# Attention values kept in DRAM by head pair, and the first value bands loaded ahead of the biases, in a hybrid encoder block

## The chip, the core and the metric

The kernel runs on one core of one Trainium2 chip. The metric is device time in microseconds (us); lower is better. A profiled execution of the same program gives the rows shown below; its span goes from the first to the last instruction.

## What is computed

The reference is one encoder block over 1024 tokens (a grid of 16 rows by 64 columns) of 1024 channels, in float32. Cut to what matters here:

```python
h = rmsnorm(x, norm_mix_g)
proj = h @ w_in                        # 1024 x 2048: u (512), q, k, v (512 each)
a = pool_mixer(u, w_pool, pool_scale)  # four groups of 128 channels
b = neighbourhood_attention(q, k, v, rpb)   # 8 heads of 64 channels
x = x + concat([a, b]) @ w_out
h = rmsnorm(x, norm_mlp_g)
x = x + square(relu(h @ w_up)) @ w_down
return rmsnorm(x, final_g)
```

In the attention each token at (row, column) attends to a window of 8 rows by 16 columns. The columns are worked in four bands of 16 query columns, whose keys and values lie in 24, 32, 32 and 24 grid columns.

## The kernel before

Every matmul is split in three: an operand is cut into a high part (a cast on ScalarE, line 100) and a low part (a subtraction on VectorE or GpSimd, line 101), and high x high, high x low and low x high go to TensorE (lines 143, 145 and 147). A weight tile therefore costs casts on ScalarE (`wh`) and subtractions on GpSimd (`wl`) before TensorE can use it.

The stages, in order of time: the norm of eight blocks of 128 tokens with the projection of the values, which `project_v` copies out of PSUM (`vs`, line 245) and stores to `vd` in DRAM; the bias tables `di` and `df`, built in SBUF and stored to DRAM; the projection of q and k for head pair 0 (`project_qk`, 24 matmuls for each half of the tokens, 96 in all); then a loop over 64 attention tiles in which TensorE works on the scores, the transposes and the values of one tile and, in between, on the projections of head pairs 1 to 3 and of the four pooling groups. After that come the output projection and the MLP, which the change doesn't touch.

`load_v(hp, j)` loads the values of head pair `hp` in band `j`: 96 or 128 partitions (4 grid rows of 24 or 32 columns) by four blocks of rows by 128 channels. `split_v` casts them into `vhl` on ScalarE and GpSimd. `load_bias` fills a bias tile with two loads; the first four tiles are eight loads, 240 and 160 KB or 300 and 120 KB for each tile. `fetch` loads a projection weight of 128 columns (512 KB), and `loaded` hands out one weight, puts the splitting of the next into the list `later`, and fetches the one after that.

All these loads are issued by SyncE (SP) on one queue. The projections use two PSUM banks in turn, so the third half-projection can't start before the first is out of its bank, and so on. What comes out is written by ScalarE (line 467 for q, line 476 for k) and VectorE (lines 468 and 477).

Up to the output projection the order on each engine isn't the order of the code: a list scheduler decides it when the program is built. Each engine then works strictly in that order, so an instruction that waits holds up all that stand behind it on its engine. SP has eight completion semaphores for its loads and uses them in turn: a load waits until the eighth load before it has landed.

Of the kernel before, what the change touches and what calls it, by code (L numbers as in the profile page):

```python
# [8 lines left out]
F32 = mybir.dt.float32  # L9
# [6 lines left out]
P = 128  # L16
T = 1024
# [3 lines left out]
HALF = 512  # L21
WINDOWS = (2, 4, 8, 16)
GW = 64
# [14 lines left out]
def block_kernel(ctx, tc, x, norm_mix_g, w_in, w_pool, pool_scale, rpb, w_out,  # L38
                 norm_mlp_g, w_up, w_down, final_g, out):
    nc = tc.nc  # L40
# [7 lines left out]
    out = out[0]  # L48
# [5 lines left out]
    dram = ctx.enter_context(tc.tile_pool(name="dram", bufs=1, space=DRAM))  # L54
# [12 lines left out]
    def bank(tag):  # L67
        return psum[0].tile([P, 512], F32, tag=tag, name=f"ps_{tag}")

    def t2(name, dt=F32):  # L70
        return k2.tile([P, 512], dt, tag="k2", name=name)

    def t4(name, dt=F32):
        return k4.tile([P, 1024], dt, tag="k4", name=name, bufs=NARROW)

    def t4w(name, n=1040):
        return k4.tile([P, 1152], F32, tag="k4w", name=name, bufs=WIDE)[:, :n]
# [4 lines left out]
    def r32(ap):  # L82
        return ap.bitcast(F32)
# [14 lines left out]
    def split(hi, lo, src, lo_eng=None):  # L98

        nc.scalar.copy(out=hi, in_=src)  # L100
        (lo_eng or nc.vector).tensor_tensor(out=lo, in0=src, in1=r32(hi), op=ALU.subtract)  # L101
# [38 lines left out]
    def three(ps, wh, wl, ah, al, first, last, more=False):  # L140


        nc.tensor.matmul(ps, wh, ah, start=first, stop=False, skip_group_check=more)  # L143
        yield
        nc.tensor.matmul(ps, wh, al, start=False, stop=False, skip_group_check=more)  # L145
        yield
        nc.tensor.matmul(ps, wl, ah, start=False, stop=last, skip_group_check=more)  # L147
        yield
# [3 lines left out]
    def step(k):  # L152

        if later and k % 4 == 0:
            later.pop(0)()
# [5 lines left out]
    def run(steps):  # L161
        for k, _ in enumerate(steps):
            step(k)
# [1 line left out]
    def quads(ts):  # L165
        return [t.rearrange("p (c t) -> p c t", c=4) for t in ts]

    vd = dram.tile([T, HALF], F32, name="vd")
    ad = dram.tile([T, D], F32, name="ad")
    di = dram.tile([8, 5, 16, KR, WSUM], F32, name="di")  # L170
    df = dram.tile([8, 8, 16, 8, WSUM], F32, name="df")
# [19 lines left out]
    with ExitStack() as pv:  # L191
# [24 lines left out]
        for i in range(4):  # L216
            raw = (t4w("wvraw", 1024) if i < WIDE else t4("wvraw")).rearrange("p (c n) -> p c n", c=2)
# [19 lines left out]
        def project_v(tt):  # L237
            tsl = slice(tt * P, (tt + 1) * P)
            ps = bank("pp")
            for c in range(NC8):  # L240
                g, k = divmod(c, 4)
                run(three(ps, hh[g][:, k, tsl], hl[g][:, k, tsl], wvh[:, c, :], wvl[:, c, :],
                          c == 0, c == NC8 - 1))
            vs = t2("vs")
            nc.scalar.copy(out=vs, in_=ps)
            nc.sync.dma_start(out=vd[tsl, :], in_=vs)

        transposed(norm_x(0), hh, hl, 0, ("S", "T"))
        for nh, ps in enumerate(gps):
# [52 lines left out]
        def loaded():  # L302

            flush()
            w = weights.pop(0)
            if weights:
                pieces(*weights[0], 2, nc.gpsimd)
            if cols:
                weights.append(fetch(cols.pop(0)))
            return w  # L310

        hn = norm_x(1)
        for tt in range(NC8):
            if tt + 1 < NC8:
                transposed(hn, hh, hl, (tt + 1) * P, ("S", "T"))
            if tt + 2 < NC8:
                hn = norm_x(tt + 2)
            project_v(tt)
            if tt == 3:
                build_tables()  # L320
            if tt == 3:
                weights.append(fetch(cols.pop(0)))
            if tt == 5:
                pieces(*weights[0], 2, nc.gpsimd)
                flush()
            if tt == 5:
                store_tables()

    def project(w, pss, chunks=range(NC8), blocked=False):

        for th, ps in pss:
            sl = slice(th * HALF, (th + 1) * HALF)
            for c in chunks:
                g, k = divmod(c, 4)
                ah, al = hh[g][:, k, sl], hl[g][:, k, sl]
                if blocked:
                    ah = ah.rearrange("p (r j c) -> p j r c", r=8, j=4)
                    al = al.rearrange("p (r j c) -> p j r c", r=8, j=4)
                yield from three(ps, w[0][:, c, :], w[1][:, c, :], ah, al, c == 0, c == NC8 - 1)
# [69 lines left out]
    with ExitStack() as pt_:  # L409
# [11 lines left out]
        def load_bias(h, e, rb):  # L421
            bt = bias[e, rb]
            if rb == 0:
                nc.sync.dma_start(out=bt[64:128], in_=di[h, 0:4].rearrange("s b r c -> (s b) r c"))
                nc.sync.dma_start(out=bt[0:64, 0:8, :], in_=df[h, 0:4].rearrange("s b r c -> (s b) r c"))
            else:
                nc.sync.dma_start(out=bt[0:80], in_=di[h].rearrange("s b r c -> (s b) r c"))
                nc.sync.dma_start(out=bt[80:128, 4:12, :], in_=df[h, 5:8].rearrange("s b r c -> (s b) r c"))

        def load_v(hp, j):  # L430
            c0, w, _ = BANDS[j]
            raw = t2("vraw").rearrange("p (c n) -> p c n", c=4)
            for c in range(4):
                src = bass.AP(vd.tensor, vd.offset + (c * 4 * GW + c0) * HALF + hp * P,
                              [[GW * HALF, 4], [HALF, w], [1, P]])
                nc.sync.dma_start(out=raw[:4 * w, c, :], in_=src)
            return raw

        def split_v(raw, j):
            w = BANDS[j][1]  # L440
            vhl = t4("vhl", F32R).rearrange("p (c s d) -> p c s d", c=4, s=4)
            split(vhl[:4 * w, :, 0:4:3, :], vhl[:4 * w, :, 1:3, :],
                  raw[:4 * w].rearrange("p c (e d) -> p c e d", e=2), lo_eng=nc.gpsimd)
            return vhl

        def tq(name):
            return qk.tile([P, T], F32R, tag="qk", name=name)

        def side(e):
            return slice(64 * e, 64 * e + 64), slice(64 - 64 * e, 128 - 64 * e)  # L450
# [3 lines left out]
        def project_qk(hp, loaded, last_first=False):  # L454
            kl = [tq("kl") for _ in range(2)]
            q1 = [tq("q1") for _ in range(2)]
            k1 = [tq("k1") for _ in range(2)]
            ready[hp] = q1, k1, kl
            wgt = loaded()
            for th in range(2):  # L460
                ps = bank("pp")
                yield from project(wgt, [(th, ps)], blocked=True)
                for e in range(2):
                    me, ot = side(e)
                    psj = ps[me].rearrange("p (j n) -> p j n", j=4)
                    q5 = q1[e].rearrange("p (j b n) -> p j b n", j=4, b=2)
                    nc.scalar.mul(out=q5[me, :, th], in_=psj, mul=-0.125)
                    nc.vector.scalar_tensor_tensor(  # L468
                        out=q5[ot, :, th], in0=psj, scalar=-0.125,
                        in1=r32(q5[me, :, th]), op0=ALU.mult, op1=ALU.subtract)  # L470

            def evac(th, ps):
                sl = slice(th * HALF, (th + 1) * HALF)
                for e in range(2):
                    me, ot = side(e)
                    nc.scalar.copy(out=k1[e][me, sl], in_=ps[me])
                    nc.vector.tensor_tensor(out=kl[e][me, sl], in0=ps[me],
                                            in1=r32(k1[e][me, sl]), op=ALU.subtract)
                    nc.sync.dma_start(out=r32(k1[e][ot, sl]), in_=r32(k1[e][me, sl]))
                    nc.sync.dma_start(out=r32(kl[e][ot, sl]), in_=r32(kl[e][me, sl]))  # L480

            wgt = loaded()
            if last_first:
                pss = [(th, bank("pp")) for th in range(2)]
                yield from project(wgt, pss, range(4))
                yield from project(wgt, pss, range(4, NC8))
                for th, ps in pss:
                    evac(th, ps)
            else:
                for th in range(2):  # L490
                    ps = bank("pp")
                    yield from project(wgt, [(th, ps)])
                    evac(th, ps)

        tiles = [(hp, j, e, rb) for hp in range(4) for j in range(4) for e in range(2) for rb in range(2)]
        bs, vraw, vhls, state = [], {}, {}, {}
# [149 lines left out]
            flush()  # L646
            yield from out_pools()

        for e in range(2):
            for rb in range(2):  # L650
                load_bias(e, e, rb)
        run(project_qk(0, loaded))
        vraw[0, 0] = load_v(0, 0)
        vhls[0, 0] = split_v(vraw[0, 0], 0)
        vraw[0, 1] = load_v(0, 1)
        fill = enumerate(filler())
        state["done"], state["acc"] = 0, acc

# [9 lines left out]
        for i in range(len(tiles) + 3):  # L668
            if i < len(tiles):
                hp, j, e, rb = tiles[i]  # L670
# [471 lines left out]
    held, c = {}, {}  # L1142
# [125 lines left out]
```

## Time and profile before

| | us |
|---|---|
| median of 3 runs | 1029.84 |
| lowest and highest run | 1028.5 and 1030.84 |
| the profiled execution's own time | 1031.89 |
| its span | 1030.1 |
| busy in the span: TensorE (PE) | 982.0 |
| VectorE (DVE) | 662.3 |
| ScalarE (ACT) | 537.7 |
| GpSimd (POOL) | 174.8 |

TensorE is busy for 95% of the span. Its mean granted clock is 0.981 of full speed. The hardware queue that SP issues to moves 157.51 MB in 103,040 packets.

### The profile page before, as it was taken

The numbers are of one execution on the slowest core, as the hardware profiler recorded it, in microseconds if no ns is written. First come the engines' busy times: TensorE is split into PE (matmuls) and PEld (weight loads), VectorE is DVE, ScalarE is ACT, GpSimd is POOL, SyncE is SP. The second block draws the span as 40 slices with busy tenths as digits, with TensorE's granted clock in tenths as the row PEclk, the third lists the DMA queues.
The fourth block names the chain that finished last, engine by engine and source line by source line (L and its number), as shares of the span: only waits on it lengthen the run. The fifth ranks groups of instructions, "written<-read, shape, count | busy, mean of one in ns | idle before, by whom it ended". The sixth has DMA issues, their size and how long they took to land.

```text
span 1030.1 us, 13174 instructions
## 1 busy us (share of the span) xinstructions
PE 982.0 (95%) x4508; PEld 811.8 (79%) x4508; DVE 662.3 (64%) x1165; ACT 537.7 (52%) x1045; POOL 174.8 (17%) x228
## 2 busy tenths in 40 slices
PE   7998999999899896599999999999999999999996
PEld 5786888887787774488888888888888888888885
DVE  6512588577665557577656656654677868649774
ACT  6413666567652545366556556555544544445463
POOL 3613436252530110000000000000020202003211
PEclk9999999999899997799999999999999999999998
DMA  8585333504761431465554554528966434355222
GB/s 290 153 236 129 76 94 82 145 23 106 247 209 75 174 132 62 133 214 175 159 171 130 158 168 123 164 82 286 341 221 229 160 104 162 103 203 186 86 102 100
DMA packets 103685, 159.40 MB, mean 155 GB/s; under 512 B 9409, under 2 KB 48833, under 8 KB 103618
## 3 DMA queue, kind: packets, MB, share of 16 engines
q1 hardware_dynamic: 103040, 157.51, 48.2%
q10 hardware_dynamic: 578, 1.05, 0.3%
q8 instruction: 35, 0.57, 0.2%
q14 instruction: 32, 0.26, 0.1%
HBM read 105.83 MB, written 48.27 MB: 150 GB/s over the span
## 4 chain that ended last, share of the span: by engine, by line
PE 83%; DMA 3%; issue 3%; DVE 3%; ACT 2%; POOL 2%; SPq 2%; ACTq 0%; POOLq 0%; DVEq 0%
PE ps_pp L143 5%; PE ps_pp L145 5%; PE ps_pp L147 5%; PE ps_a L145 5%; PE ps_a L143 5%; PE ps_a L147 5%; PE ps_x L147 4%; PE ps_b L145 4%; PE ps_b L143 4%; PE ps_b L147 4%; PE ps_x L143 4%; PE ps_x L145 4%; PE ps_w L143 3%; PE ps_w L145 3%; PE ps_w L147 3%
## 5 line engine op out<-in xcount | busy, mean ns | idle before, releaser
L100 ACT CAST st<-ur 128x512 fp32r<-128x512 f32 x112 | 69.7, 622 | 133.0 <-PE ps_a L147 61.4
L101 DVE TENSOR_TENSOR st<-ur,st 128x512 fp32r<-128x512 f32 x112 | 82.8, 739 | 80.8 <-ACT st L100 80.3
L1130 POOL TENSOR_TENSOR m<-m,x2t 128x512 f32<-128x512 f32 x16 | 27.3, 1729 | 519.0 <-DMA x2t<-x 402.3
L147 PE MATMUL ps_a<-st 128*128 128x512 f32 x256 | 99.7, 390 | 0.0
L143 PE MATMUL ps_a<-st 128*128 128x512 f32 x256 | 99.7, 389 | 0.0
L145 PE MATMUL ps_a<-st 128*128 128x512 f32 x256 | 99.7, 389 | 0.0
L101 DVE TENSOR_TENSOR st<-pq,st 128x512 fp32r<-128x512 f32 x112 | 84.5, 754 | 1.1
L143 PE MATMUL ps_pp<-hh,wh 128*128 128x512 f32 x192 | 76.7, 399 | 2.0 <-DVE q L468 2.0
L145 PE MATMUL ps_pp<-hl,wh 128*128 128x512 f32 x192 | 76.6, 399 | 0.0
L147 PE MATMUL ps_pp<-hh,wl 128*128 128x512 f32 x192 | 76.4, 398 | 0.0
L100 ACT CAST st<-pq 128x512 fp32r<-128x512 f32 x112 | 69.0, 616 | 13.6 <-DVE pq L1077 13.5
L143 PE MATMUL ps_b<-st 128*128 128x512 f32 x192 | 74.8, 390 | 0.0
L145 PE MATMUL ps_b<-st 128*128 128x512 f32 x192 | 74.8, 389 | 0.0
L147 PE MATMUL ps_b<-st 128*128 128x512 f32 x192 | 74.8, 389 | 0.0
L855 ACT ACTIVATE r<-r 128x512 f32<-128x512 f32 x64 | 40.5, 632 | 65.0 <-DVE r L736 65.0
L143 PE MATMUL ps_x<-hop,s 128*128 128x512 f32 x180 | 70.2, 390 | 0.0
L145 PE MATMUL ps_x<-hop,s 128*128 128x512 f32 x180 | 70.1, 390 | 0.0
L147 PE MATMUL ps_x<-hop,s 128*128 128x512 f32 x180 | 70.1, 389 | 0.0
L528 POOL TENSOR_SCALAR s<-s,ri 128x288 f32<-128x288 f32 (+1 forms) x64 | 42.5, 667 | 109.8 <-DVE ri L527 87.3
L143 PE MATMUL ps_w<-hop,s 128*128 128x512 f32 x128 | 50.7, 396 | 10.4 <-ACT s L741 10.4
L728 DVE TENSOR_TENSOR s<-wraw,s 128x512 fp32r<-128x512 f32 x74 | 50.5, 686 | 8.6 <-ACT s L741 8.3
L143 PEld LDWEIGHTS ps_a<-st 128*128 128x128 f32 x256 | 48.1, 188 | 10.0
(216 smaller groups left out, 2438.5 us busy)
## 6 DMA issues: line engine op xcount, KB each, us to landing
ur<-us SPq DMA_DIRECT2D x56, 512.0 KB
us<-r SPq DMA_DIRECT2D x64, 256.0 KB
wraw<-in_w_up_dram SPq DMA_DIRECT2D x16, 1024.0 KB
pq<-in_w_down_dram SPq DMA_DIRECT2D x32, 512.0 KB
us<-s SPq DMA_DIRECT2D x48, 256.0 KB
xt<-in_x_dram SPq DMA_DIRECT2D x15, 512.0 KB
wraw<-in_w_in_dram SPq DMA_DIRECT2D x12, 512.0 KB
woraw<-in_w_out_dram SPq DMA_DIRECT2D x8, 512.0 KB
```

The costliest lines, as they stand in the source:

```text
L100: nc.scalar.copy(out=hi, in_=src)
L101: (lo_eng or nc.vector).tensor_tensor(out=lo, in0=src, in1=r32(hi), op=ALU.subtract)
L143: nc.tensor.matmul(ps, wh, ah, start=first, stop=False, skip_group_check=more)
L145: nc.tensor.matmul(ps, wh, al, start=False, stop=False, skip_group_check=more)
L147: nc.tensor.matmul(ps, wl, ah, start=False, stop=last, skip_group_check=more)
L528: nc.gpsimd.tensor_scalar(out=s[:, :n], in0=s[:, :n], scalar1=ri, scalar2=1.0, op0=ALU.mult, op1=ALU.mult)
L728: lows.append((key, lambda: nc.vector.tensor_tensor(out=lo, in0=src, in1=r32(hi), op=ALU.subtract)))
L855: nc.scalar.activation(out=r, in_=r, func=AF.Relu)
L1130: nc.gpsimd.tensor_tensor(out=c[tt], in0=c[tt], in1=x, op=ALU.add)
```

## The change

`vd` is no longer kept as token by channel, but as head pair, place in a block of four grid rows (4 x 64 tokens), block of rows, channel. A band of one head pair then needs, for each of its 96 or 128 tokens of a block, one run of 512 floats that holds all four blocks of rows. So `load_v` makes one transfer with 2 KB for each partition in place of four with 512 bytes, and there are 16 transfers in place of 64. The stores of `vd` write four runs of 512 bytes for each partition in place of one of 2 KB. In the code, the first two bands stand ahead of the projection of q and k for head pair 0, and the eight loads of the first biases stand after its 25th step.

```diff
-    vd = dram.tile([T, HALF], F32, name="vd")
+    vd = dram.tile([4, 4 * GW, 4, P], F32, name="vd")
...
-            nc.sync.dma_start(out=vd[tsl, :], in_=vs)
+            nc.sync.dma_start(out=vd[:, tt % 2 * P:(tt % 2 + 1) * P, tt // 2, :].rearrange("h p d -> p h d"),
+                              in_=vs.rearrange("p (h d) -> p h d", h=4))
...
             raw = t2("vraw").rearrange("p (c n) -> p c n", c=4)
-            for c in range(4):
-                src = bass.AP(vd.tensor, vd.offset + (c * 4 * GW + c0) * HALF + hp * P,
-                              [[GW * HALF, 4], [HALF, w], [1, P]])
-                nc.sync.dma_start(out=raw[:4 * w, c, :], in_=src)
+            src = bass.AP(vd.tensor, vd.offset + (hp * 4 * GW + c0) * HALF,
+                          [[GW * HALF, 4], [HALF, w], [1, HALF]])
+            nc.sync.dma_start(out=raw[:4 * w].rearrange("p c n -> p (c n)"), in_=src)
...
-        for e in range(2):
-            for rb in range(2):
-                load_bias(e, e, rb)
-        run(project_qk(0, loaded))
         vraw[0, 0] = load_v(0, 0)
+        vraw[0, 1] = load_v(0, 1)
         vhls[0, 0] = split_v(vraw[0, 0], 0)
-        vraw[0, 1] = load_v(0, 1)
+        for k, _ in enumerate(project_qk(0, loaded)):
+            step(k)
+            if k == 24:
+                for e in range(2):
+                    for rb in range(2):
+                        load_bias(e, e, rb)
```

The scheduler answers with an order of its own. On ScalarE, in the projection of the values, this stands before the change (`wh_486` is the high part of the k weights of head pair 0, `wh_710` that of the q weights of pair 1, `hn` and `hh` belong to the norm and the transposed activations):

```order
L118 ACTIVATE hn_425,ssq_426<-xt_177 128x1024
L100 CAST wh_486<-wraw_484 128x512 x2
L100 CAST wh_710<-wraw_708 128x512 x2
L245 COPY vs_408<-ps_pp_383 128x512
L100 CAST hh_133<-ps_S_411 128x4x128
```

And this after it:

```order
L118 ACTIVATE hn_425,ssq_426<-xt_177 128x1024
L246 COPY vs_408<-ps_pp_383 128x512
L100 CAST hh_133<-ps_S_411 128x4x128
L100 CAST hh_135<-ps_T_418 128x4x128
L118 ACTIVATE hn_502,ssq_503<-xt_179 128x1024
```

The casts of both weights have left this place, and with them their low parts on GpSimd. They now stand where the first q is taken out of PSUM. There ScalarE had, before the change, from the last block of values on (`q1_704` and `q1_705` are the q of pair 0, twice, for each half of the tokens; `k1` its k; `wh_776` the k weights of pair 1, `wh_881` those of a pooling group):

```order
L245 COPY vs_671<-ps_pp_646 128x512
L467 ACTIVATE q1_704<-ps_pp_712 64x4x128
L467 ACTIVATE q1_705<-ps_pp_712 64x4x128
L100 CAST vhl_853<-vraw_848 96x4x2x64
L100 CAST wh_776<-wraw_774 128x512 x2
L467 ACTIVATE q1_704<-ps_pp_745 64x4x128
L100 CAST vhl_910<-vraw_856 128x4x2x64
L467 ACTIVATE q1_705<-ps_pp_745 64x4x128
L100 CAST wh_881<-wraw_879 128x512 x2
L476 CAST k1_706<-ps_pp_778 64x512
```

After the change it has (`wh_486` as above, `wh_709` and `wh_783` the q and k weights of pair 1, `wh_875` the pooling group):

```order
L246 COPY vs_671<-ps_pp_646 128x512
L100 CAST vhl_698<-vraw_694 96x4x2x64
L468 ACTIVATE q1_703<-ps_pp_711 64x4x128
L100 CAST wh_486<-wraw_484 128x512 x2
L468 ACTIVATE q1_704<-ps_pp_711 64x4x128
L100 CAST wh_709<-wraw_707 128x512 x2
L468 ACTIVATE q1_703<-ps_pp_744 64x4x128
L100 CAST wh_783<-wraw_781 128x512 x2
L468 ACTIVATE q1_704<-ps_pp_744 64x4x128
L100 CAST vhl_904<-vraw_696 128x4x2x64
L100 CAST wh_875<-wraw_873 128x512 x2
L477 CAST k1_705<-ps_pp_785 64x512
```

The first band now stands ahead of the first q, and four weights, where there were two, stand between the first q and the first k.

On SP the loads stood like this before the change, from the last store of values on (`wraw_708` and `wraw_774`, the q and k weights of pair 1, had been fetched long before):

```order
L246 DMA vd_121<-vs_671 128x512
L424 DMA bias00_686<-di_123 64x960
L425 DMA bias00_686<-df_124 64x640
L427 DMA bias01_688<-di_123 80x960
L428 DMA bias01_688<-df_124 48x640
L424 DMA bias10_690<-di_123 64x960
L425 DMA bias10_690<-df_124 64x640
L427 DMA bias11_692<-di_123 80x960
L428 DMA bias11_692<-df_124 48x640
L436 DMA vraw_848<-vd_121 96x1x128 x3
L436 DMA vraw_856<-vd_121 128x1x128 x4
L184 DMA wraw_879<-in_w_in_dram 128x8x128
```

After it, from the third load of biases on:

```order
L429 DMA bias01_688<-di_123 80x960
L437 DMA vraw_694<-vd_121 96x1x512
L437 DMA vraw_696<-vd_121 128x1x512
L430 DMA bias01_688<-df_124 48x640
L426 DMA bias10_690<-di_123 64x960
L185 DMA wraw_707<-in_w_in_dram 128x8x128
L427 DMA bias10_690<-df_124 64x640
L429 DMA bias11_692<-di_123 80x960
L430 DMA bias11_692<-df_124 48x640
L185 DMA wraw_781<-in_w_in_dram 128x8x128
L437 DMA vraw_907<-vd_121 128x1x512
L437 DMA vraw_1057<-vd_121 96x1x512
```

The next load there is `wraw_873`, the weight of the pooling group. The first two bands have moved ahead of five of the eight bias loads, and the q and k weights of pair 1 have come into this stretch, behind the bands and among the biases.

## Rows read from the trace of the kernel before

**Rows 1.** The page, busy time of each engine in us, share of the span.

```profile
PE 982.0 (95%) x4508; PEld 811.8 (79%) x4508; DVE 662.3 (64%) x1165; ACT 537.7 (52%) x1045; POOL 174.8 (17%) x228
```

**Rows 2.** Timeline of PE: start, us, instruction; in brackets idle before, and releaser.

```profile
39.92 0.50 PE L143 MATMUL ps_pp<-wvh,hh 128*128 128x512 f32 x1 [0.84 <-ACT hh L100]
46.44 0.63 PE L136 MATMUL ps_S<-ident,hn 128*128 128x128 f32 x4 [0.51 <-DVE hn L127]
64.60 0.40 PE L143 MATMUL ps_pp<-hh,wh 128*128 128x512 f32 x1
76.08 0.39 PE L143 MATMUL ps_pp<-hh,wh 128*128 128x512 f32 x1
83.72 0.47 PE L143 MATMUL ps_pp<-hh,wh 128*128 128x512 f32 x1 [2.01 <-DVE q L468]
89.28 0.40 PE L143 MATMUL ps_pp<-hh,wh 128*128 128x512 f32 x1
97.68 0.50 PE L506 MATMUL ps_S<-k,q 128*128 128x288 f32 x2 [2.51 <-DMA kl<-kl]
```

**Rows 3.** Timeline of ACT, 37 to 85 us.

```profile
37.76 1.14 ACT L100 CAST wh<-wraw 128x512 fp32r<-128x512 f32 x2 [8.26 <-DMA wraw<-in_w_in_dram]
...
77.91 0.62 ACT L100 CAST vhl<-vraw 96x512 fp32r<-96x512 f32 x1 [5.44 <-DMA vraw<-vd]
...
81.61 0.62 ACT L100 CAST vhl<-vraw 128x512 fp32r<-128x512 f32 x1 [1.42 <-DMA vraw<-vd]
82.26 0.59 ACT L467 ACTIVATE q<-ps_pp 64x512 fp32r<-64x512 f32 x1
...
84.42 0.58 ACT L476 CAST k<-ps_pp 64x512 fp32r<-64x512 f32 x1
```

**Rows 4.** Timeline of POOL, 38 to 45 us.

```profile
38.76 2.51 POOL L101 TENSOR_TENSOR wl<-wraw,wh 128x512 fp32r<-128x512 f32 x2
...
44.40 0.58 POOL L112 TENSOR_TENSOR rs<-ms,mhalf 128x1 f32<-128x1 f32 x1
```

**Rows 5.** Timeline of DVE, 82 to 87 us.

```profile
82.88 0.69 DVE L468 SCALAR_TENSOR_TENSOR q<-ps_pp,q 64x512 fp32r<-64x512 f32 x1 [1.98 <-ACT q L467]
...
86.37 0.70 DVE L477 TENSOR_TENSOR kl<-ps_pp,k 64x512 fp32r<-64x512 f32 x1 [0.65 <-ACT k L476]
```

**Rows 6.** Timeline of SP's queue: start, us in the issuing instructions.

```profile
33.08 1.19 SPq L184 DMA_DIRECT2D wraw<-in_w_in_dram  x2
...
65.45 0.32 SPq L246 DMA_DIRECT2D vd<-vs  x1
...
70.76 6.03 SPq L436 DMA_DIRECT2D vraw<-vd  x7
...
95.11 0.48 SPq L480 DMA_DIRECT2D kl<-kl  x1
```

**Rows 7.** Windows: busy us of each engine, granted clock, DMA share, GB/s.

```profile
50.00:52.00 2.00, 2.00 (x11) 1.65 (x10) 0.00 (x0) 0.00 (x0) 0.00 (x0) 1.00 1.02 361
66.00:74.40 8.40, 8.40 (x36) 6.65 (x35) 1.38 (x2) 1.18 (x2) 2.24 (x3) 1.00 0.97 220
...
388.00:392.00 4.00, 1.78 (x10) 1.21 (x9) 3.56 (x5) 2.23 (x5) 0.00 (x0) 1.00 0.66 197
392.00:396.00 4.00, 4.00 (x16) 3.29 (x15) 3.92 (x8) 1.76 (x3) 0.00 (x0) 0.60 0.01 4
```

**Rows 8.** DMA from 75.2 to 78.4 us; share of the sixteen engines.

```profile
DMA packets 498, 0.25 MB, mean 77 GB/s; under 512 B 17, under 2 KB 498, under 8 KB 498
...
q1 hardware_dynamic: 498, 0.25, 31.8%
```

**Rows 9.** DMA from 78.4 to 80.4 us.

```profile
DMA packets 980, 0.49 MB, mean 247 GB/s; under 512 B 14, under 2 KB 980, under 8 KB 980
...
q1 hardware_dynamic: 980, 0.49, 105.7%
```

## The prediction, made before the changed kernel was run

> **What bounds the kernel now.** I read the page first: TensorE is busy for 982.0 of 1030.1 us [rows 1], so what counts is where it waits and who lets it go. The timeline of PE shows that ahead of the output projection it waits four times for longer than half a microsecond once the values are being projected, all before 98 us [rows 2]: 0.84 us for a high part on ScalarE, 0.51 us for a norm, 2.01 us for q to leave its PSUM bank, 2.51 us for copies of k. From there to about 240 us it has no wait, and the later stages hang on TensorE's progress, so a shift before 98 us should reach the end whole. The time of the change is decided in this stretch.
>
> The other engines' timelines say what stands behind each wait. At 37.76 us ScalarE casts weights of which the second pair was fetched only at 33.08 us, and has sat idle for 8.26 us [rows 3, 6]; that is the 0.84 us. Behind them GpSimd works off the low parts (2.51 us for two) and reaches the norm's factor only at 44.40 us [rows 4]; that is the 0.51 us. At 77.91 us ScalarE starts on the first band after 5.44 us of idleness, at 81.61 us on the second after 1.42 us more, and the last q of pair 0 stands behind both [rows 3]; that is the 2.01 us. The copies of k are issued at 95.11 us, among loads of bands; that is the 2.51 us.
>
> **What the change removes.** The two weights' casts leave the projection of the values. The 0.84 and 0.51 us should go: the high part that TensorE waited for could have been made right after its transpose, and the low parts no longer stand ahead of the norm. That is -1.35 us, in all cases below.
>
> **What a band costs, the disputed price.** Between 75.2 and 78.4 us nothing but bands moves: 498 packets of 512 bytes at 77 GB/s, with 31.8% of the sixteen engines [rows 8]. Between 78.4 and 80.4 us weights move too, in packets of the same size: 980, at 247 GB/s and 105.7% [rows 9]. A packet holds its engine equally long in both (0.318 x 16 x 3.2 us / 498 = 33 ns; 1.057 x 16 x 2.0 us / 980 = 35 ns). So the bands aren't slow because their packets are small; some five engines work, where the weights have all sixteen. And SP had issued seven of these transfers by 76.8 us [rows 6], so it wasn't for want of work.
>
> The new transfer could cost by packets, which are four times fewer: 96 at 156 per us are 0.62 us, 128 are 0.82. Or it keeps to few engines and costs by bytes: 192 KB at 77 GB/s are 2.55 us, 256 KB are 3.4. Four of sixteen engines at the best rate of this stage, 361 GB/s [rows 7], would give 90 GB/s, so 2.2 and 2.9 us. I take these last two. The source of both forms walks over four grid rows first, and I see nothing that would spread the new one over more engines; the longer pieces speak for the faster end.
>
> The Trainium skill has a rule for this (DMA: Bandwidth & Descriptors, "Why a DMA increments its semaphore by 16 and not by 1"): a transfer runs on the largest number of engines up to sixteen that divides the slowest dimension of both of its sides. With four grid rows against 96 or 128 partitions that gives four engines, before the change and after it. The trace agrees for the form before (31.8%, about five), and no run yet shows the form after. By this rule the sum is the one that I take; by packets alone it is that of the first rival.
>
> **What is moved.** In the new order ScalarE casts the first band ahead of the first q, and between there and the first k four weights instead of two, each behind a load; in the loads' queue the bands stand ahead of most biases, and the weights behind both. Before, the two weights of pair 1 had landed long ago. I follow the loads on the few engines that the bands use, which do them one after the other, with 64.60 us as zero: the first matmul of q [rows 2].
>
> The last store of values is issued at 65.45 us, 0.85 after zero. The store and the eight biases took from about 66 to 74.4 us at 220 GB/s [rows 7], so the store's 256 KB are through at about 2.6. Biases go at 220 GB/s, weights of 512 KB at 247 GB/s (2.1 us), and a load is of use some 1.6 us after its last packet: before the change the first band's last 288 packets follow the biases at 74.4 us, at 156 per us until 76.25, and its cast starts at 77.91.
>
> - Three bias loads (700 KB, 3.3 us) to 5.9; first band 2.2 to 8.1; of use at 9.7. Then ScalarE and VectorE need the band's cast 0.62, q 0.59, two casts of weights 1.14, q 0.59, and VectorE's q 0.69 [rows 3, 5]: 3.6. The bank is free at 13.3, where the k projection of pair 0 starts; before at 76.08, so 11.5.
> - Second band 2.9 to 11.0; two biases (360 KB, 1.7) to 12.7; first weights to 14.8; three biases (580 KB, 2.7) to 17.5; second weights to 19.6; of use at 21.2. Casts 1.14, q 0.59, VectorE 0.69: at 23.6 the second half of k starts. The first half was done at 18.8, so TensorE has waited 4.8; before at 83.72, so 19.1.
> - Third band 2.9 and fourth 2.2 to 24.7; third weights to 26.8; of use at 28.4. Casts 1.14, then the first half of k out of its bank, which takes 2.65 (from 84.42 to 87.07 [rows 3, 5]): at 32.2 the q of pair 1 starts. The second half of k was done at 29.1. Before at 89.28, so 24.7.
> - One half-projection is 5.7 (64.60 to 76.08 are two), so the first scores could start at 37.9; before at 97.68, so 33.1. The copies of k pass behind two more bands and another weight and land about then; that wait of 2.51 us has gone into the longer ones.
>
> The sum: 37.9 - 33.1 = +4.8, and -1.35, is **+3.4 us**. Made against the profiled span of 1030.1 us (1031.89 with what lies around it) it stays a difference; on the median of 1029.84 us it gives **1033.2 us**.
>
> Edits that I put at nothing: the stores of values, in four runs each. The last store lands before the three biases ahead of the first band have passed (5.9), and these are its cover; if it took a microsecond longer than they do, the first band and all behind it would move by what is over. The 48 fewer transfers on SP: its queue is seldom what TensorE waits for, and after 98 us there is no wait to shorten.
>
> **Rivals.** *The bands cost by packets* (0.62 and 0.82 us), which ends on the faster side. The first k then starts at 11.7, the second weights are of use at 17.5 and the second half of k starts at 19.9, the third weights are of use at 21.1, early enough: q of pair 1 follows at 25.4 and the scores at 31.1. That is 2.0 us earlier than before, with the 1.35 us 3.3 us, so 1026.5 us. For it: the transfers are fewer and their packets longer. Against it: the share in rows 8. It decides if a band takes less than about 1.3 us; from there up the weights' landings are what TensorE waits for.
>
> *The loads are faster all round.* Bands at 2.0 and 2.7 us, weights at 1.75 us (300 GB/s), biases at 250 GB/s: the third weights are through at 23.9 and not 26.8, the scores start at 35.0, so +1.9 - 1.35 = +0.5 us, 1030.4 us, no change. For it: the queue has peaks of 361 GB/s [rows 7]. Against it: the biases held 220 GB/s for 8.4 us.
>
> *The clock falls as well.* Between 388 and 392 us TensorE was idle for 2.2 of 4 us, and in the next four the granted clock was 0.60, so it spent part of them at the lower of its two levels [rows 7]: 1.6 us lost. The wait of 4.8 us is longer than that one. What the lower clock takes from the second half of k is hidden by the wait behind it; after the second wait (3.1 us) it would cost another 1.6 us: 1034.8 us. I count this case into the forecast's.
>
> **Chances and range.** The forecast with its clock case 0.55, packets 0.20, faster loads 0.25. The difference that a measurement of this kernel can tell from none is about 0.2%, or 2.1 us. So faster 0.20, same 0.25, slower 0.55. With bands at 77 GB/s the four that count add 0.35 + 0.5 + 0.5 + 0.35 = 1.7 us, so +5.1, and the clock's 1.6 us make 1036.5: the likeliest case's own range is 1031 to 1036.5 us. The whole range reaches down to the packets' case, 1026 to 1036.5 us.
>
> **What would show it.** In the profile of the changed kernel: no wait of TensorE at 40 and 46 us, and q of pair 0 starting about 1.35 us earlier; a stretch with bands alone still at a third of the engines, with packets of 2 KB; ScalarE idle ahead of three pairs of weight casts, its releaser a load of `w_in`; TensorE waiting about 2, 5 and 3 us for VectorE's q and kl; the first scores some 3.4 us later than 97.68 us. The forecast falls if a band moves with nearly all engines, if the weights land before the bands, or if a stretch after 98 us gets waits of its own, for which I see no cause.

## The result, and the profile after the change

The changed kernel takes 1036.73 us (median of 5 runs, 1034.91 to 1040.29), the kernel before 1030.68 us beside it; the ratio is 1.0057, 95% interval 1.0039 to 1.0075. It is slower by some 6 us: the sign of the forecast, nearly twice its size, and 0.2 us outside its range. (The range was worked out from a median of 1029.84 us for the kernel before; beside the changed kernel it took 0.84 us more.) The profiled run is the slowest of the five (1040.29 us, mean granted clock 0.976; the other four have 0.981 to 0.983), so the terms read from it add up to 8.4 us and not to 6.

The page's first part, answering to [rows 1]: TensorE is busy for 3 us more, and the span is 8.4 us longer, so most of the loss is waiting.

```profile
PE 985.2 (95%) x4508; PEld 814.2 (78%) x4508; DVE 659.6 (64%) x1165; ACT 536.8 (52%) x1045; POOL 163.0 (16%) x228
```

The timeline of PE, answering to [rows 2]. There is no wait left at 40 and 46 us, and the first q starts 1.17 us earlier; then come four waits where there were two.

```profile
63.43 0.40 PE L143 MATMUL ps_pp<-hh,wh 128*128 128x512 f32 x1
...
76.20 0.48 PE L143 MATMUL ps_pp<-hh,wh 128*128 128x512 f32 x1 [1.13 <-DVE q L469]
...
87.71 0.77 PE L143 MATMUL ps_pp<-hh,wh 128*128 128x512 f32 x1 [5.77 <-DVE q L469]
...
96.28 0.47 PE L143 MATMUL ps_pp<-hh,wh 128*128 128x512 f32 x1 [1.22 <-DVE kl L478]
...
104.02 0.50 PE L507 MATMUL ps_S<-k,q 128*128 128x288 f32 x2 [1.77 <-DMA kl<-kl]
```

The timeline of ACT, answering to [rows 3]: ahead of the first q stands the cast of the first band, which waits for its load, and ahead of the later q and of k stands each time a weight's cast that waits for its load, the q and k weights of pair 1 at 81.74 and 85.08 us, the pooling weight at 92.33 us.

```profile
72.57 0.62 ACT L100 CAST vhl<-vraw 96x512 fp32r<-96x512 f32 x1 [8.32 <-DMA vraw<-vd]
...
81.74 1.14 ACT L100 CAST wh<-wraw 128x512 fp32r<-128x512 f32 x2 [6.41 <-DMA wraw<-in_w_in_dram]
82.90 0.59 ACT L468 ACTIVATE q<-ps_pp 64x512 fp32r<-64x512 f32 x1
85.08 1.14 ACT L100 CAST wh<-wraw 128x512 fp32r<-128x512 f32 x2 [1.59 <-DMA wraw<-in_w_in_dram]
...
92.33 1.14 ACT L100 CAST wh<-wraw 128x512 fp32r<-128x512 f32 x2 [4.85 <-DMA wraw<-in_w_in_dram]
```

DMA from 87.3 to 89.3 us, answering to [rows 8], with nothing but a band moving: 94 packets of 2 KB and 4 short ones, a quarter of the engines.

```profile
DMA packets 98, 0.19 MB, mean 96 GB/s; under 512 B 4, under 2 KB 4, under 8 KB 98
...
q1 hardware_dynamic: 98, 0.19, 26.3%
```

The chain of waits up to the first scores: the last weight takes 13.32 us from its issue, a copy of k is issued only when it has landed, and its low part lands 2.26 us after that.

```profile
87.84 13.32 DMA wraw<-in_w_in_dram
101.22 0.46 SPq L480
101.78 2.26 DMA kl<-kl
```

Windows (columns as in [rows 7]): up to 108 us the granted clock falls twice, in the wait of 5.77 us and at the first scores, after the wait of 1.77 us; 0.60 over 4 us means that most of it lies at the lower level, 1.2 GHz.

```profile
84.00:88.00 4.00, 0.29 (x1) 0.33 (x2) 0.90 (x2) 2.35 (x4) 3.14 (x3) 0.54 0.70 171
88.00:92.00 4.00, 4.00 (x12) 3.12 (x12) 0.00 (x0) 0.00 (x0) 1.50 (x2) 0.60 0.40 119
...
104.00:108.00 4.00, 3.98 (x13) 3.36 (x14) 0.49 (x3) 0.22 (x1) 0.00 (x0) 0.60 0.00 1
```

### The profile page after: what moved, and what is told of

It reads as the page before. It is cut to its first block, busy times and chain, and to the rows that moved or that the text cites. A ratio compares the mean times of both kernels' runs of the same rounds, so it can differ in the third digit from the quotient of the medians.

```text
span 1038.5 us, 13088 instructions
## 1 busy us (share of the span) xinstructions
PE 985.2 (95%) x4508; PEld 814.2 (78%) x4508; DVE 659.6 (64%) x1165; ACT 536.8 (52%) x1045; POOL 163.0 (16%) x228
## 4 chain that ended last, share of the span: by engine, by line
PE 81%; DMA 4%; DVE 3%; ACT 2%; issue 2%; SPq 1%; POOL 1%; ACTq 0%; POOLq 0%; DVEq 0%
PE ps_a L145 5%; PE ps_a L143 5%; PE ps_a L147 5%; PE ps_pp L147 5%; PE ps_pp L145 5%; PE ps_pp L143 5%; PE ps_x L147 4%; PE ps_b L147 4%; PE ps_b L145 4%; PE ps_b L143 4%; PE ps_x L143 4%; PE ps_x L145 4%; PE ps_w L143 3%; PE ps_w L145 3%; PE ps_w L147 3%; DMA wraw<-in_w_in_dram 2%
## 5 line engine op out<-in xcount | busy, mean ns | idle before, releaser
L101 DVE TENSOR_TENSOR st<-pq,st 128x512 fp32r<-128x512 f32 x112 | 81.1, 724 | 1.0
L145 PEld LDWEIGHTS ps_a<-st 128*128 128x128 f32 x256 | 48.0, 188 | 10.1
L143 PEld LDWEIGHTS ps_a<-st 128*128 128x128 f32 x256 | 48.0, 188 | 10.0
```

## The experiments

Each time stands beside runs of the kernel before on the same chip; the ratio is to those.

| run | median, us | ratio (95% interval) |
|---|---|---|
| layout_alone | 1037.18 | 1.0058 (1.0043 to 1.0072) |
| order_alone | 1034.95 | 1.0042 (1.0029 to 1.0056) |
| split_48 | 1034.94 | 1.0033 (1.0014 to 1.0051) |
| by_rows | 1029.63 | 0.9985 (0.9972 to 0.9997) |
| weight_first | 1034.99 | 1.0041 (1.0027 to 1.0055) |
| layout_rows | 1027.53 | 0.9970 (0.9960 to 0.9980) |
| rows_48 | 1027.83 | 0.9976 (0.9959 to 0.9993) |
| kcopy_pool | 1040.60 | 1.0103 (1.0087 to 1.0118) |
| warm | 1034.23 | 1.0044 (1.0030 to 1.0059) |
| split48_wf | 1035.61 | 1.0048 (1.0030 to 1.0066) |
| change_wf | 1035.01 | 1.0049 (1.0034 to 1.0065) |
| layout_pool_last | 1028.82 | 0.9980 (0.9969 to 0.9991) |
| change_pool_last | 1030.69 | 1.0000 (0.9987 to 1.0014) |
| rows_pool_last | 1024.00 | 0.9936 (0.9924 to 0.9949) |
| rows48_pool_last | 1024.61 | 0.9936 (0.9919 to 0.9952) |
| before_pool_last | 1030.15 | 0.9996 (0.9982 to 1.0010) |

**Half of the change at a time.** `layout_alone` is the kernel before with the new `vd`, its stores and the one-transfer band; `order_alone` is the change with these three put back.

```diff
-    vd = dram.tile([T, HALF], F32, name="vd")
+    vd = dram.tile([4, 4 * GW, 4, P], F32, name="vd")
```

> Only the layout of vd and the one-transfer bands; bands and biases stand in the code as before the change. Theory A (displaced weights: the loss comes from the weights of pair 1 landing behind the first bands): within 2 us of before, so 1029 to 1032.5, with both weights fetched near 33 us and first scores at 96 to 98 us. Theory B (the layout itself costs: stores in four runs, bands of 2 KB packets on few engines): most of the 6 us, 1034 to 1037.

> Only the code order (first two bands ahead, biases after the 25th step); vd is token by channel, a band is four transfers. Theory A: the weights of pair 1 are displaced here too, so 1033 to 1038, with waits of TensorE for q of pair 0. Theory B: as before the change, 1029 to 1032.

Theory A fell on the first: the layout alone is as slow as the whole change, with both weights of pair 1 fetched early. Its timelines of PE and ACT show one long wait, of 9.01 us, for q behind a weight's cast:

```profile
90.44 0.76 PE L143 MATMUL ps_pp<-hh,wh 128*128 128x512 f32 x1 [9.01 <-DVE q L468]
```

```profile
81.13 0.62 ACT L100 CAST vhl<-vraw 128x512 fp32r<-128x512 f32 x1 [2.09 <-DMA vraw<-vd]
81.77 0.59 ACT L467 ACTIVATE q<-ps_pp 64x512 fp32r<-64x512 f32 x1
87.82 1.14 ACT L100 CAST wh<-wraw 128x512 fp32r<-128x512 f32 x2 [5.45 <-DMA wraw<-in_w_in_dram]
88.98 0.59 ACT L467 ACTIVATE q<-ps_pp 64x512 fp32r<-64x512 f32 x1
```

and its SP queue, that four bands are issued ahead of that weight, where before there were two:

```profile
70.38 2.57 SPq L436 DMA_DIRECT2D vraw<-vd  x4
73.09 2.82 SPq L184 DMA_DIRECT2D wraw<-in_w_in_dram  x1
```

The weight is the first pooling weight. The order that the scheduler wrote has changed here too: before, ScalarE had `q1_704`, `vhl_910`, `q1_705`, `wh_881`, so that this cast stood behind both q; now, as its rows above show, it has the second band, q, the weight, q.

DMA from 80 to 83 us in this run, with all four bands issued: they do not run beside each other on other engines.

```profile
DMA packets 143, 0.28 MB, mean 94 GB/s; under 512 B 6, under 2 KB 6, under 8 KB 143
...
q1 hardware_dynamic: 143, 0.28, 25.8%
```

`order_alone` is slower too, as theory A said and theory B did not, but by other waits: 4.25 us for a low part of k, and 2.13 us for a q at the first scores (read from an execution of 1032.26 us).

```profile
89.74 0.77 PE L143 MATMUL ps_pp<-hh,wh 128*128 128x512 f32 x1 [4.25 <-DVE kl L478]
```

So either half costs most of what both cost together.

**The weights of pair 1.** They had left their early place because the cast of the first band now takes, in the order of the code, the buffer that the first of them used to take. `split_48` allocates it later, and both weights are fetched early again.

```diff
-        vhls[0, 0] = split_v(vraw[0, 0], 0)
         for k, _ in enumerate(project_qk(0, loaded)):
             step(k)
+            if k == 48:
+                vhls[0, 0] = split_v(vraw[0, 0], 0)
```

> The change, with the cast of the first band allocated after the 49th step of the first projection, so that the weights of pair 1 get the buffers that they had before and are fetched early again. Theory A: most of the loss goes, 1031 to 1034; ScalarE's block near 38 us comes back, and what is left is the second band and the pooling weight ahead of the second q (k's second half about 22 us after the first q matmul; 24.3 in the change). Theory C (the first bands ahead of the first q are the cost, whatever the weights do): as the change, 1035.5 to 1038.

The median, 1034.9, lies between what the two theories gave, 0.9 us above A's. The wait for q is still 5.24 us, now behind the pooling weight. The displaced weights are a part at most.

**The engines of a band.** `by_rows` is the change with a band in four transfers, one for each grid row; `layout_rows` the layout alone with them; `rows_48` is `split_48` with them.

```diff
-            src = bass.AP(vd.tensor, vd.offset + (hp * 4 * GW + c0) * HALF,
-                          [[GW * HALF, 4], [HALF, w], [1, HALF]])
-            nc.sync.dma_start(out=raw[:4 * w].rearrange("p c n -> p (c n)"), in_=src)
+            for r in range(4):
+                src = bass.AP(vd.tensor, vd.offset + (hp * 4 * GW + r * GW + c0) * HALF, [[HALF, w], [1, HALF]])
+                nc.sync.dma_start(out=raw[r * w:(r + 1) * w].rearrange("p c n -> p (c n)"), in_=src)
```

> The change, with a band fetched as four transfers of one grid row each (24 or 32 tokens of 2 KB) in place of one over four grid rows. Theory A with few engines as the price: a band moves with 12 to 16 engines, above 200 GB/s, takes about 1 us, the weights land 4 to 5 us earlier against the first q matmul, and the time is 1025.5 to 1030. Rival (the bands' price does not matter, the place of the weights behind the biases does): 1034 to 1037.

> The new layout alone, with a band fetched as four transfers of one grid row each; code order as before the change. By the price of few engines: a band takes about 1 us, the pooling weight stands behind two bands and lands near 80 us, the wait for q of pair 0 is under 1 us, and the time is 1026.5 to 1030. Rival (with the order of before the engines of a band do not matter): 1030 to 1032.

> The change, with a band as four transfers of one grid row each, and the first band's cast allocated after the 49th step, so that the weights of pair 1 are fetched early. If both repairs are needed and add: waits of TensorE before the first scores under 2 us in all, 1025.5 to 1029. If the spread over the engines alone is what counts: 1029 to 1031, as with the rows alone.

The times of `by_rows` and `layout_rows` lie where the price of few engines had them, that of `rows_48` where both repairs add, but waits are left: 2.14 us for q in `layout_rows`, 2.00 us in `rows_48`, and 4.04 us for a low part of k in `by_rows`, behind the casts of the k weights of pair 1 and the pooling weight. What the early weights of `rows_48` add to the rows isn't settled, since its interval overlaps that of `by_rows`. DMA from 75.5 to 76.5 us in `layout_rows`, where only bands move:

```profile
DMA packets 130, 0.17 MB, mean 174 GB/s; under 512 B 45, under 2 KB 45, under 8 KB 130
...
q1 hardware_dynamic: 130, 0.17, 93.3%
```

The bytes, the packet size and the stores are those of `layout_alone`; the engines go from 25.8% to 93.3% and the rate from 94 to 174 GB/s, less than the 200 that I had expected. The Trainium skill (DMA: Bandwidth & Descriptors, "Why a DMA increments its semaphore by 16 and not by 1") would give a row of 24 or 32 tokens 12 or 16 engines, and the trace agrees. The rows also bring the scheduler back to two bands ahead of the pooling weight, so these runs don't separate the engines from the place (two runs further down do); theory B (the stores, or 2 KB packets, cost by themselves) is out, since both are in `layout_rows`, which is 3 us faster than before.

**The place of the pooling weight in the queue.** One element of the weight is copied into the third band's buffer ahead of its load, so that the band waits for the weight: in `weight_first` with the layout alone, in `change_wf` with the change, in `split48_wf` with `split_48`.

```diff
             raw = t2("vraw").rearrange("p (c n) -> p c n", c=4)
+            if (hp, j) == (0, 2):
+                nc.gpsimd.tensor_copy(out=raw[0:1, 0, 0:1], in_=weights[-1][2][0:1, 0, 0:1])
```

> The new layout alone, with the third band made to wait for the pooling weight (one element of it is copied into the band's buffer ahead of the load), so that the queue has two bands, then the weight, where the layout alone has four bands ahead of it. Theory D (place in the queue: the third and fourth band, 448 KB on few engines, hold up the pooling weight that the second q stands behind): the weight lands about 5 us earlier, the wait of 9.0 us for q falls to 3 to 5 us, 1029.5 to 1032.5. Theory B (stores in four runs or the 2 KB packets cost by themselves): 1035 to 1038, as the layout alone.

> The change, with only the third band made to wait for the pooling weight. Theory D: the waits of 1.1 and 5.8 us for q stay (the weights of pair 1 stand ahead of those bands anyway), the waits of 1.2 us for k and 1.8 us for its copies go, 1033 to 1035. Rival (the place of those bands matters only where the weights of pair 1 are early): 1036 to 1037.5.

> The change, with the first band's cast allocated after the 49th step and the third band made to wait for the pooling weight: both of the displaced groups of weights are back in front, bands still on few engines. Theory A and D together: the wait of 5.2 us for q (left with the split alone) falls to 2 to 3.5 us, 1030 to 1032.5. Rival (each alone is all there is to have): 1034 to 1036.

Theory D had too much in it. In `weight_first` the weight is of use at 83.98 us, 3.8 us earlier, but its cast has moved ahead of both q of the second half, and the wait is still 6.20 us (read from an execution of 1031.68 us, 3.3 us under the median); the ratio falls from 1.0058 to 1.0041, with intervals that overlap. `change_wf` came to the upper end of its forecast (1035.0): the wait for k has gone, the one for the copies has not (1.85 us). `split48_wf` missed: 1035.6, with the cast at 84.85 us ahead of both q; the weight is no earlier there than in `split_48` (83.76 us), where only two bands stood ahead of it already. Being earlier in the queue helps little as long as q stands behind the cast.

**The pooling weight's cast out of the way.** What it makes is needed late: the first half of its projection is copied out of PSUM at 137.5 us in the change. In these runs its load waits for the last low part of k of pair 0, so that the scheduler puts the cast behind all of q and k.

```diff
         raw = t4("wraw").rearrange("p (c n) -> p c n", c=NC8)
+        if col == 3 * P:
+            nc.gpsimd.tensor_copy(out=raw[64:65, 0, 0:1], in_=r32(ready[0][2][1][64:65, 512:513]))
         nc.sync.dma_start(out=raw, in_=w_in[:, col:col + P]
```

> The new layout alone, bands of one transfer, with the load of the first pooling weight made to wait for the last low part of k of head pair 0 (one element of it is copied into the weight's buffer ahead of the load), so that its cast on ScalarE stands behind all of q and k of pair 0. Theory G (with the new layout it is this cast, put ahead of q's last evacuation while its load stands behind bands on few engines, that TensorE waits for): the wait of 9.0 us for q is under 1 us, 1026 to 1029.5. Rival (the layout costs by itself): 1034 to 1038.

> The change, with the same delay of the first pooling weight. Theory G with A: what is left is the q weight of pair 1, cast at 81.7 us ahead of the second q, so the wait of 5.8 us falls to about 3, that of 1.2 us for k goes, 1029 to 1032.5. Rival (the weights of pair 1 are the whole loss): 1035 to 1037.

> The new layout alone, bands as four transfers of one grid row each, with the same delay of the first pooling weight. Theory G: the wait of 2.1 us for q that the rows alone have goes too, 1024.5 to 1027. Rival (its place goes to the copies of k): 1027 to 1028.5.

> The change with all three repairs: rows, the first band's cast allocated after the 49th step, the first pooling weight delayed. Theory: no wait for q, 1023.5 to 1026.5. Rival (its place goes to the copies of k): 1026.5 to 1028.5.

> The kernel before the change, with only the first pooling weight delayed as in the three runs of that kind. If the gain of the best version is the delay's alone: 1024 to 1026, as the rows with the delay. If each has its part: the wait of 2.0 us for q goes, the one of 2.5 us for the copies of k stays, 1027 to 1029.5, and layout and rows together are worth some 3 to 5 us on top.

Theory G held, in times and waits, and `rows_pool_last` came half a microsecond under its forecast. With the bands still on few engines, the layout alone goes from 1.0058 to 0.9980 and the change from 1.0057 to 1.0000. In the timeline of PE of `layout_pool_last` only the wait for the copies of k is left between the first q and the scores:

```profile
95.39 0.60 PE L508 MATMUL ps_S<-k,q 128*128 128x288 f32 x2 [2.52 <-DMA kl<-kl]
```

and in `change_pool_last` waits for q, the long one behind the q weight of pair 1, that is, part of what the displaced weights cost:

```profile
75.43 0.47 PE L143 MATMUL ps_pp<-hh,wh 128*128 128x512 f32 x1 [0.97 <-DVE q L471]
...
84.95 0.47 PE L143 MATMUL ps_pp<-hh,wh 128*128 128x512 f32 x1 [3.81 <-DVE q L471]
```

The delay moved more than the one cast. The cast of the k weights of pair 1 now stands behind q and k too: at 94.24 us in `change_pool_last`, for 85.08 us in the change, where q had waited behind it; at 89.11 us in `layout_pool_last`, for 77.91 us in `layout_alone`, where it had its weights already. And the loads of the pooling weight and of the one behind it no longer stand ahead of the copies of k. In `layout_alone` the long wait was behind the pooling weight's cast alone; for the change these runs don't separate the three.

`rows_pool_last`, without the change's new code order, beats both kernels: 1024.00 us, 0.9936. From 40.16 us on, its TensorE has no wait above a quarter of a microsecond until

```profile
238.24 0.62 PE L550 MATMUL ps_O<-pth,vhl 128*128 128x256 f32 x3 [0.90 <-DVE pth L101]
```

It and `layout_pool_last` separate the engines from the place: in both, six bands and no weight stand ahead of the copies of k in SP's queue, the code differs in the rows alone, and the intervals of the ratios lie apart. With bands on few engines the chain of waits of `layout_pool_last` goes through a band to the copy of k that the first scores wait for; `rows_pool_last` has no such wait.

```profile
79.87 12.91 DMA vraw<-vd
...
92.84 2.38 DMA kl<-kl
```

The delay alone (`before_pool_last`) changes nothing that can be measured, which neither case had expected: the wait for q goes, but the one for the copies of k stays, 2.60 us at 95.47 us. So the layout cut by rows is what is worth having, once the casts are out of its way. How much of that the new layout has by itself is open: the intervals of `layout_pool_last` and `before_pool_last` overlap, and no run cuts the old `vd` by grid rows.

**The copies of k.** In `kcopy_pool`, the change, GpSimd issues them in place of SP.

```diff
-                    nc.sync.dma_start(out=r32(k1[e][ot, sl]), in_=r32(k1[e][me, sl]))
-                    nc.sync.dma_start(out=r32(kl[e][ot, sl]), in_=r32(kl[e][me, sl]))
+                    nc.gpsimd.dma_start(out=r32(k1[e][ot, sl]), in_=r32(k1[e][me, sl]))
+                    nc.gpsimd.dma_start(out=r32(kl[e][ot, sl]), in_=r32(kl[e][me, sl]))
```

> The change, with the copies of k between partitions issued by GpSimd in place of SP. Theory E (in the change the copies are held in SP's queue behind bands and weights, eight loads in turn): the wait of 1.77 us ahead of the first scores goes, and the low clock behind it, 1033.5 to 1035.5. Rival (the copies take that long by themselves, or GpSimd is busy): 1036 to 1038.5.

The kernel is slower (1.0103), outside both ranges. Ahead of the first scores 1.13 us are left, for which the profile names no copy, but the loss comes back later, in the timeline of PE:

```profile
264.80 0.50 PE L143 MATMUL ps_pp<-woh,msp 128*128 128x512 f32 x1 [3.88 <-ACT woh L100]
```

Another order of all engines came with this edit, so the price of SP's queue by itself stays open; that SP held the copies back for a weight is shown by the chain above.

**The clock.** `warm` is the change with 24 extra matmuls, whose result nothing reads, in TensorE's longest wait.

```diff
+        warm = bank("T")
...
+            if k == 71:
+                for n in range(24):
+                    nc.tensor.matmul(warm, hh[0][:, 0, 0:P], ready[0][0][0][:, 0:512], start=True, stop=True)
```

> The change, with 24 extra matmuls (their result goes to a PSUM bank that nothing reads) between the first and the second half of k of head pair 0, where TensorE waits 5.8 us; everything else keeps its order. Theory F (part of the loss is the clock that falls after the wait): the second half of k starts at the same time, its matmuls keep 0.39 us, and 1.5 to 2.5 us come back: 1034 to 1035.3. Rival (the clock costs nothing here, only the waits do): 1036 to 1037.5.

They start late, after a wait of 1.69 us for q, and end at 89.8 us, so the second half of k starts 2 us later than in the change. All the same the scores come 0.9 us earlier, and the granted clock stays up. Its timeline of PE and its windows:

```profile
84.02 5.78 PE L658 MATMUL ps_T<-q,hh 128*128 128x512 f32 x24 [1.69 <-DVE q L469]
...
103.15 0.51 PE L507 MATMUL ps_S<-k,q 128*128 128x288 f32 x2 [1.14 <-DMA k<-k]
```

```profile
88.00:92.00 4.00, 4.00 (x19) 3.30 (x19) 0.00 (x0) 0.00 (x0) 1.30 (x2) 1.00 0.46 136
...
104.00:108.00 4.00, 4.00 (x19) 3.25 (x18) 1.78 (x7) 1.15 (x4) 0.54 (x2) 1.00 0.00 0
```

So the idle engine is what the clock falls after, and theory F is right about the trace. The time, 1034.2 us, lies in its range, but the interval of the ratio (1.0030 to 1.0059) overlaps that of the change (1.0039 to 1.0075): how much it is worth in the median isn't settled.

## Why the prediction was right and wrong

**The early waits.** Forecast -1.35 us, measured -1.17 (63.43 for 64.60 us): right.

**The price of a band.** It keeps to a quarter of the engines, at 96 GB/s where I took 90: right, and the rival that it costs by packets is out. A clear advantage of the layout appeared only when I gave the band its engines (`layout_rows`, `rows_pool_last`).

**The waits for q and k.** From the first q matmul, I had the first half of k at 13.3 us, the second at 23.6 and the q of pair 1 at 32.2; the profile has 12.8, 24.3 and 32.9. The waits are 1.13, 5.77 and 1.22 us (forecast about 2, 5 and 3), behind the loads named. Following the loads one after the other on few engines was right.

**The step that failed** is the last of the sum: "The copies of k pass behind two more bands and another weight and land about then; that wait of 2.51 us has gone into the longer ones." It had not: 1.77 us of it are still there. A copy is issued only when the eighth load before it has landed, and for the fourth copy of k's high part, whose data was ready at 97.46 us, that is a weight that lands just ahead of 101.22 us; the sum had no term for it. So the scores come 40.6 us after zero and not 37.9. Of these 2.7 us, 0.65 were already there when the q of pair 1 started, 1.77 are the wait, and the rest is 0.3.

**The clock** I had put ahead only as an extra of 1.6 us. In the profiled run it falls twice up to 108 us. The first fall is hidden by the wait for k behind it, as I said; the second, from 104 to 108 us, costs up to 1.6 us (40% of 4 us). With a later wait for copies of k (1.74 us at 273.9 us, before 0.31), and less for a weight of the output projection (0.72 for 1.32), it brings the +6.3 us at the scores to the +8.4 us of that run. Which part of this the median run, at +6.05 us, doesn't have, no trace shows; its mean granted clock, 0.983 for 0.976, says that it spent less time at the lower level.

**What I had not seen** is which of the causes is enough by itself. I put the loss down to the weights of pair 1 and to bands on few engines. But each half of the change costs most of the whole: in either a weight's cast that waits for its load comes to stand ahead of q or k of pair 0 (9.01 us of waiting for q, 4.25 for k), and the two losses don't add. The order listings of the change already showed the pooling weight's cast ahead of k; I counted its 3.1 us and did not ask whether anybody needed it then. Delaying that weight gives back all that the change had lost (`change_pool_last`, 1.0000), though the q weight of pair 1 still costs a wait of 3.81 us there: the earlier start, and the wait for the copies of k ahead of the first scores, which is gone, pay for it.

**The other rivals.** Faster loads all round (1030.4 us) is out: the second and third weights were of use half a microsecond after the sum's times (21.65 for 21.2 us, 28.9 for 28.4), the first weights 1.9 us after. A stretch after 98 us with waits of its own was named as what would upset the forecast, and there is one: the copies of k for a later pair.

## What to carry to other kernels

One large transfer in place of four small ones is no gain if its slowest dimension is four: look at the share of the engines first, and cut it so that each piece spreads over many of them. Each piece has to be issued, though: in `rows_pool_last` SP takes 13.19 us over 22 of them, and from 78 to 80 us, while it issues five, only 46.9% of the engines are in use, at 129 GB/s. When an edit makes transfers fewer, ask a list scheduler's order what it now puts ahead of what: here two more bands got ahead of a weight, and the weight's cast ahead of q, on engines that work strictly in order. A cast of something needed tens of us later doesn't belong between a PSUM bank and the matmul that waits for it; and moving an allocation of a shared pool forward takes a buffer away from whatever was fetched early into it.

SP's queue in `rows_pool_last`:

```profile
70.91 13.19 SPq L438 DMA_DIRECT2D vraw<-vd  x22
```

## What the runs showed of the hardware

Packets, nearly all of 2 KB, held their engine for 86 ns on average when a band ran alone on few engines (0.263 x 16 x 2.0 us / 98). When bands ran on nearly all of them it was 115 ns, with short packets making up a third (0.933 x 16 x 1.0 us / 130): 3.5 times the share of the engines gave 1.8 times the rate.

A load of 512 KB behind bands on few engines took 13.32 us from issue to landing in the change, where 2.1 us would do at the 247 GB/s of [rows 9]. Shortly before it landed, from 99 to 100.5 us, nearly all packets were of under 2 KB, as a weight's are (some may be of a 64 KB load behind it), and a third of the engines was in use:

```profile
DMA packets 218, 0.12 MB, mean 79 GB/s; under 512 B 5, under 2 KB 212, under 8 KB 218
...
q1 hardware_dynamic: 218, 0.12, 32.8%
```

So the last part of the weight came on few engines. That these are the engines of the bands fits their share (31.8% in [rows 8], with packets of the same size), but the profile doesn't name engines.
